# Ten of the eighteen projections of the dilated attention as five units of seven half-size products

## The chip, the cores and the metric

The kernel runs on one core of a Trainium2 chip. The metric is device time in microseconds (us) from the first to the last instruction, with what lies around them. Five engines work side by side, each through its own list of instructions in a fixed order: TensorE (PE in the profile, with its weight loads as PEld), VectorE (DVE), ScalarE (ACT), GpSimd (POOL) and SyncE (SP), which here only issues transfers.

## The reference

A two-layer encoder over 512 tokens of width 1024. The first layer feeds two head groups from one projection; the change concerns group B:

```
z = rmsnorm(x, mix_norm_ab[i]) @ w_in_ab[i]
o_a = mla_mixer(z[..., :IN_A], mla_q_norm[i], mla_kv_norm[i], w_uq, w_ukv, cos_t, sin_t)
o_b = dilated_mixer(z[..., IN_A:], slopes)
x = x + jnp.concatenate([o_a, o_b], axis=-1) @ w_out_ab[i]
...
# dilated_mixer: h_b columns are [q | k | v], each ordered (group, slot, dim): 3 groups, 4 slots, 64 dims
outs.append(o); lses.append(lse)          # one banded attention for each of the 3 groups
comb = sum(softmax(lses)[..., None] * outs)
```

Everything is in float32. The second layer has grouped-query attention, and each layer ends in a SwiGLU FFN.

## The kernel before, in words

Activations lie transposed: a tile holds 128 of the 1024 features in its partitions and the 512 tokens in its columns; eight such tiles make the input of a projection. Each float32 operand is split into a high part (rounded, by ACT) and a low part (the rest, a subtraction on DVE or POOL), and a product is three matmuls, high by high, high by low and low by high (`mm3`, L166 to L168). A projection of 128 output columns (`proj`) is thus 8 x 3 = 24 matmuls with 512 columns each. Its weights come by `load`: one transfer into one of two `wraw` tiles, a cast on ACT (`whi`, L155), a subtraction on POOL (`wlo`, L156).

At the start the input is turned on PE, scaled and split into `x0` to `x15` (`Norm.feed`, L208 and L209). Each tile is also squared on ACT (L199), and POOL adds the squares up into `nacc` (L203). From that sum comes the norm's row factor: four short matmuls sum over the partitions (`rsqrt`, L221), DVE adds the epsilon (L224), POOL raises to the power -0.5 (`rcol`, L226), PE spreads the factor over all partitions (`spread`, L233), and ACT copies it to `rbc` (L237). Only then can a projection's result leave PSUM, since the instruction that takes it out multiplies it by `rbc` (L408, L415, L458, L463, L470, L473, L477). While `rbc` is missing, the banks of PSUM fill up: `BANKS` gives two banks to "acc", two to "s", three to "pt" and one to "o".

The order of the work: the latent projections of head group A (two in the first phase, three by `wblock`); then for each of two values of `sp` the nine projections of the dilated attention (q, k, v for three groups; 128 columns are two slots), then the eight score tiles of these two slots (`steps.tile`, which has a higher priority). After that come group A's heads, the output projection and the FFN. The program is written in this order, but the framework then orders each engine's instructions by a timeline of its own, so that later projections stand between earlier score tiles.

The FFN already works by units of seven (class `Seven`): two projections over 1024 features are a 2 x 2 block product and are formed from seven products of half the depth (4 tiles) and half the columns (256), 7 x 4 x 3 = 84 matmuls with 256 columns, out of sums of the weights (`sab`, `sdc`, split on ACT and DVE) and sums of the activations (`sums`, made once for a set of units).

Of the kernel before, what the change touches and what calls it, by code (L numbers as in the profile page):

```python
# [94 lines left out]
def encoder_kernel(ctx: ExitStack, tc: tile.TileContext, a, out):  # L95
# [349 lines left out]

    for sp in range(2):
        def block(which, g):
            col = IN_A + 768 * which + g * 256 + sp * P
            return proj(wblock(col), xs)

        q1 = [U(f"d{j}", F32R) for j in range(2)]
        k1 = [U(f"d{2 + j}", F32R) for j in range(2)]
        k2 = [U(f"d{4 + j}", F32R) for j in range(2)]
        v0 = [U(f"d{10 + b}", F32R).rearrange("p (c j d) -> p c j d", c=2, j=2) for b in range(2)]
        qf, kf, vf = {}, {}, {}
        o = block(0, 0)
        e = E()
        nc.vector.scalar_tensor_tensor(e, o, 0.125, rbc, op0=ALU.mult, op1=ALU.mult)  # L458
        for j in range(2):
            stack(q1[j], e, j)  # L460
        o = block(1, 0)
        e = E()
        nc.vector.tensor_mul(e, o, rbc)  # L463
        for j in range(2):
            stack(k1[j], e, j)
            swap(k2[j], k1[j])
        for g in (1, 2):
            o = block(0, g)
            qf[g] = U(f"d{5 + g}")
            nc.vector.scalar_tensor_tensor(qf[g], o, 0.125, rbc, op0=ALU.mult, op1=ALU.mult)  # L470
            o = block(1, g)
            kf[g] = U(f"d{7 + g}")
            nc.vector.tensor_mul(kf[g], o, rbc)  # L473
        for g in range(3):
            o = block(2, g)
            e = E()
            nc.vector.tensor_mul(e, o, rbc)  # L477
            pt = psum("pt")
            for c in range(NT):
                nc.tensor.transpose(pt[:, c * P:(c + 1) * P], e[:, c * P:(c + 1) * P], ident)  # L480
            if g == 0:
                pw = pt.rearrange("p (c j d) -> p c j d", c=NT, j=2)
                for b in range(2):
                    split(v0[b][:, :, :, 0:64], v0[b][:, :, :, 64:128], pw[:, 2 * b:2 * b + 2])
            else:
                vf[g] = U(f"d{11 + g}")
                nc.scalar.copy(vf[g], pt)
        if sp == 0:
            finish_latents()
# [177 lines left out]

    H = T // 2  # L670
    NAMES = ("b11", "b21", "b22", "t1", "t2", "t3", "t4")

    def sums(cb, ya, yb, temps, b11, b2, t12_to, t34_to):

        t12, t34 = temps
        nc.vector.tensor_sub(t12[:, 0:H], ya[:, H:T], ya[:, 0:H])
        nc.vector.tensor_sub(t12[:, H:T], yb[:, H:T], t12[:, 0:H])
        nc.vector.tensor_sub(t34[:, 0:H], ya[:, 0:H], t12[:, H:T])
        nc.vector.tensor_sub(t34[:, H:T], yb[:, 0:H], t12[:, H:T])
# [6 lines left out]
        for j, (src, (h, l)) in enumerate(((t12, t12_to), (t34, t34_to))):  # L686
            nc.scalar.activation(h, src, AF.Copy, scale=-1.0)
            nc.vector.scalar_tensor_tensor(l, src, -1.0, h.bitcast(F32), op0=ALU.mult, op1=ALU.subtract)  # L688
            for q in range(2):
                cb[f"t{2 * j + q + 1}"].append((h[:, q * H:q * H + H], l[:, q * H:q * H + H]))  # L690
# [15 lines left out]

    class Seven:

        count = 0

        def __init__(self, loads, cb):
            self.cb = cb
            par = Seven.count % 2
            Seven.count += 1
            self.w = w = len(cb["b11"]) * P
            rg = U("wraw", bufs=2, shape=(P, WCOLS))[:, 0:2 * w]
# [1 line left out]
            at = {"g": rg, "g1": rg[:, 0:w], "g2": rg[:, w:], "u1": u1, "u2": u2}
            for name, v in loads:
                nc.sync.dma_start(at[name].rearrange("p (k n) -> p k n", n=P), v)  # L720
            g1, g2 = at["g1"], at["g2"]
            sab = U("tab", shape=(P, 2, T)).rearrange("p a b -> p (a b)")[:, 0:2 * w]
            sdc = U("bias", shape=(P, 9 * P))[:, 0:2 * w]
# [1 line left out]
            nc.vector.tensor_add(sab[:, 0:w], u1, u2)
            nc.vector.tensor_add(sab[:, w:], sab[:, 0:w], g1)
            self.a = self.parts(sab)
            nc.vector.tensor_add(sdc[:, 0:w], sab[:, w:], g2)
            nc.vector.tensor_add(sdc[:, w:], u1, g1)
            self.d = self.parts(sdc)  # L730
            uh, ul = U("oT", F32R, bufs=2)[:, 0:w], U(("m12", "otmp")[par], F32R)[:, 0:w]
            nc.scalar.copy(uh, u2)  # L732
            nc.gpsimd.tensor_sub(ul, u2, uh.bitcast(F32))  # L733
            self.u = uh, ul

        def parts(self, src):
            hi, lo = (U(t, F32R, bufs=3, shape=(P, WCOLS))[:, 0:2 * self.w] for t in ("whi", "wlo"))
            split(hi, lo, src)
            return hi, lo

        def product(self, o, w, half, name, first):
            n = len(self.cb[name])
            for i in range(n):
                c = slice(half * self.w + i * P, half * self.w + (i + 1) * P)
                x = self.cb[name][i]
                for j, (wt, xp) in enumerate(((w[0], x[0]), (w[0], x[1]), (w[1], x[0]))):
                    nc.tensor.matmul(o[:, 0:H], lhsT=wt[:, c], rhs=xp, start=first and i == 0 and j == 0,  # L747
                                     stop=i == n - 1 and j == 2, skip_group_check=True)

        def run(self, second, third, seventh, fourth):  # L750


            r1, e = psum("s"), U("p", bufs=3, shape=(P, 6 * P))
            self.product(r1, self.g, 0, "b11", True)
            nc.scalar.copy(e[:, 0:H], r1[:, 0:H])
            yield
            r2 = psum("acc")
            self.product(r2, self.g, 1, "b21", True)
            second(r2[:, 0:H], e)
            r3 = psum("pt")  # L760
            self.product(r3, self.a, 0, "t1", True)
            nc.scalar.copy(e[:, T:T + H], r3[:, 0:H])
            self.product(r1, self.a, 1, "t2", False)
            nc.scalar.copy(e[:, H:T], r1[:, 0:H])
            self.product(r3, self.d, 0, "b22", False)
# [404 lines left out]
```

## Time and profile before

| | before |
|---|---|
| median of 3 runs | 1237.79 us (1237.49 to 1238.12) |
| the profiled execution | 1237.33 us, span 1235.4 us |
| PE busy | 1215.1 us, 98% of the span |
| DVE, ACT, POOL busy | 952.4, 682.3, 464.2 us (77%, 55%, 38%) |
| granted clock of TensorE, mean | 0.997 of full speed |

The profile is one execution, recorded by the hardware. Matmuls are pipelined, so that the busy time of PE overlaps itself; what one matmul costs in a stream is read from the starts of its neighbours. A row of a timeline gives start, duration, engine, line, operation and tiles, and in brackets how long the engine sat idle before it and what it waited for.

### The profile page before, as it was taken

What the parts mean: (1) busy time and instruction counts of PE and PEld (TensorE: products, weight loads), DVE (VectorE), ACT (ScalarE), POOL (GpSimd) and SP (SyncE); (2) the same over time, 40 slices, a digit from 0 to 9 for tenths busy, and PEclk for the clock granted to TensorE, in tenths of its full rate; (3) what the DMA queues carried; (4) which work ended last, traced back from release to release, by engine and by line L of the source; (5) the groups of instructions that cost most, each with busy time, mean ns of one, the idle gap of its engine ahead of it and who ended that gap; (6) DMA issues with size and microseconds to landing.
All of it is one profiled execution on the core that took longest, in us unless ns stands there. A gap on an engine that the chain in (4) does not pass through costs nothing.

```text
span 1235.4 us, 20931 instructions
## 1 busy us (share of the span) xinstructions
PE 1215.1 (98%) x7787; PEld 1078.4 (87%) x7787; DVE 952.4 (77%) x1727; ACT 682.3 (55%) x1223; POOL 464.2 (38%) x347
## 2 busy tenths in 40 slices
PE   9999999999999999999999999999999999999997
PEld 7887788777778999999998877787788999999996
DVE  4633437983894999999965768988596799999984
ACT  5424437783653565455545467777454556456554
POOL 4544334444624022111124587756734122111210
PEclk9999999999999999999999999999999999999999
DMA  9343323223213433333424332113232333343331
GB/s 285 95 102 88 92 59 88 79 57 96 85 54 113 118 103 103 103 103 89 118 71 141 99 94 48 44 34 92 73 94 86 111 103 103 104 117 98 103 111 69
DMA packets 204725, 118.20 MB, mean 96 GB/s; under 512 B 17186, under 2 KB 196432, under 8 KB 204624
## 3 DMA queue, kind: packets, MB, share of 16 engines
q1 hardware_dynamic: 202848, 113.70, 32.6%
q10 hardware_dynamic: 1776, 3.17, 0.7%
q8 instruction: 61, 1.00, 0.3%
q14 instruction: 40, 0.33, 0.1%
HBM read 106.09 MB, written 4.19 MB: 89 GB/s over the span
## 4 chain that ended last, share of the span: by engine, by line
PE 84%; DVE 9%; DMA 2%; POOL 2%; issue 1%; ACT 1%; SPq 0%; POOLq 0%; DVEq 0%; ACTq 0%
PE ps_s L747 22%; PE ps_pt L747 11%; PE ps_acc L166 9%; PE ps_acc L167 8%; PE ps_acc L168 8%; PE ps_acc L747 6%; PE ps_pt L352 3%; PE ps_s L168 1%; PE ps_s L166 1%; PE ps_s L167 1%; PE ps_o L380 1%; PE ps_o L379 1%; PE ps_pt L168 1%; DVE b L182 1%; PE ps_pt L166 1%
## 5 line engine op out<-in xcount | busy, mean ns | idle before, releaser
L156 POOL TENSOR_TENSOR wlo<-wraw,whi 128x1024 fp32r<-128x1024 f32 (+3 forms) x99 | 184.9, 1871 | 174.6 <-ACT whi L155 163.2
L155 ACT CAST whi<-wraw 128x1024 fp32r<-128x1024 f32 (+3 forms) x106 | 87.9, 832 | 131.1 <-PE ps_acc L167 69.6
L733 POOL TENSOR_TENSOR m<-m,oT 128x512 fp32r<-128x512 f32 (+1 forms) x26 | 49.0, 1883 | 245.4 <-ACT oT L732 245.4
L166 PE MATMUL ps_acc<-x,whi 128*128 128x512 f32 x280 | 111.6, 401 | 1.9 <-DVE x L371 0.8
L168 PE MATMUL ps_acc<-x,wlo 128*128 128x512 f32 x280 | 112.0, 400 | 0.0
L167 PE MATMUL ps_acc<-x,whi 128*128 128x512 f32 x280 | 111.9, 400 | 0.0
L747 PE MATMUL ps_s<-x,whi 128*128 128x256 f32 x576 | 106.4, 282 | 0.0
L733 POOL TENSOR_TENSOR otmp<-m,oT 128x512 fp32r<-128x512 f32 (+1 forms) x26 | 42.3, 1626 | 153.0 <-ACT oT L732 149.1
L182 DVE TENSOR_TENSOR b<-ps_pt,b 128x512 fp32r<-128x512 f32 x112 | 75.0, 682 | 18.7 <-ACT b L181 18.4
L747 PEld LDWEIGHTS ps_s<-x,whi 128*128 128x128 f32 x576 | 88.8, 188 | 0.4
L181 ACT CAST whi<-bias 128x1024 fp32r<-128x1024 f32 (+1 forms) x52 | 52.8, 1016 | 58.5 <-PE ps_s L747 31.4
L747 PE MATMUL ps_s<-x,wlo 128*128 128x256 f32 x288 | 81.0, 281 | 0.0
L181 ACT CAST b<-ps_pt 128x512 fp32r<-128x512 f32 x112 | 63.7, 585 | 28.1 <-PE ps_pt L352 27.4
L181 ACT CAST whi<-tab 128x1024 fp32r<-128x1024 f32 (+1 forms) x52 | 53.0, 1019 | 46.5 <-PE ps_s L747 36.0
L166 PEld LDWEIGHTS ps_acc<-x,whi 128*128 128x128 f32 x280 | 52.5, 188 | 14.0 <-ACT e L1035 1.2
L182 DVE TENSOR_TENSOR wlo<-bias,whi 128x1024 fp32r<-128x1024 f32 (+1 forms) x52 | 61.1, 1176 | 4.1 <-ACT whi L181 3.4
L182 DVE TENSOR_TENSOR wlo<-tab,whi 128x1024 fp32r<-128x1024 f32 (+1 forms) x52 | 62.5, 1202 | 2.2 <-ACT whi L181 2.2
L182 DVE TENSOR_TENSOR wlo<-wraw,whi 128x1024 fp32r<-128x1024 f32 (+1 forms) x52 | 63.0, 1211 | 0.7 <-ACT whi L181 0.7
L167 PEld LDWEIGHTS ps_acc<-x,whi 128*128 128x128 f32 x280 | 52.7, 188 | 12.3 <-POOL x L373 0.5
L181 ACT CAST whi<-wraw 128x1024 fp32r<-128x1024 f32 (+1 forms) x52 | 52.8, 1015 | 18.2 <-PE ps_acc L167 8.6
L168 PEld LDWEIGHTS ps_acc<-x,wlo 128*128 128x128 f32 x280 | 52.8, 188 | 11.4
L747 PE MATMUL ps_pt<-x,whi 128*128 128x256 f32 x288 | 54.3, 282 | 1.8 <-DVE x L688 1.8
(497 smaller groups left out, 4015.5 us busy)
## 6 DMA issues: line engine op xcount, KB each, us to landing
wraw<-in_ffn_w_in_dram SPq DMA_DIRECT2D x52, 512.0 KB, 3.8
m<-in_ffn_w_in_dram SPq DMA_DIRECT2D x72, 256.0 KB, 3.3
wraw<-in_w_in_ab_dram SPq DMA_DIRECT2D x21, 512.0 KB, 3.9
wraw<-in_ffn_w_out_dram SPq DMA_DIRECT2D x40, 256.0 KB, 2.8
m<-in_ffn_w_out_dram SPq DMA_DIRECT2D x16, 256.0 KB, 3.5
wraw<-in_gqa_w_q_dram SPq DMA_DIRECT2D x8, 512.0 KB, 4.0
m<-in_ffn_w_out_dram SPq DMA_DIRECT2D x16, 192.0 KB, 3.4
wraw<-in_ffn_w_out_dram SPq DMA_DIRECT2D x16, 192.0 KB, 2.9
```

The source lines that it names most:

```text
L155: nc.scalar.copy(h, r)
L156: (low or nc.gpsimd).tensor_sub(l, r, h.bitcast(F32))
L166: nc.tensor.matmul(dst, lhsT=lhs[0], rhs=rhs[0], start=first, stop=False)
L167: nc.tensor.matmul(dst, lhsT=lhs[0], rhs=rhs[1], start=False, stop=False)
L168: nc.tensor.matmul(dst, lhsT=lhs[1], rhs=rhs[0], start=False, stop=last)
L181: nc.scalar.copy(hi, src)
L182: nc.vector.tensor_sub(lo, src, hi.bitcast(F32))
L352: nc.tensor.transpose(pt[:, k * P:(k + 1) * P], p[:, k * P:(k + 1) * P], ident)
L379: nc.tensor.matmul(o, lhsT=vs[k][:, h, :], rhs=pth[:, k, :], start=k == 0, stop=False)
L380: nc.tensor.matmul(o, lhsT=vs[k][:, h, :], rhs=ptl[:, k, :], start=False, stop=k == NT - 1)
L733: nc.gpsimd.tensor_sub(ul, u2, uh.bitcast(F32))
L747: nc.tensor.matmul(o[:, 0:H], lhsT=wt[:, c], rhs=xp, start=first and i == 0 and j == 0, stop=i == n - 1 and j == 2, skip_group_check=True)
```

## The change

The eighteen projections of the dilated attention were nine for `sp` 0, then nine for `sp` 1. Now the first two (q and k of group 0 for `sp` 0) stay as they are, ten others become five units of `Seven`, all written ahead of the first score tile (`PAIRS`), and six of `sp` 1 stay where they were. Three of the ten belong to `sp` 1 (`EARLY_W`); their results wait in `first` and `nacc`. The sums of the activations that the units need are made by the new `window_inputs`, which adds high and low part of `x` again on POOL (`ya`, `yb`), forms four differences of 128 x 256 on DVE for each of four pairs of tiles, and splits them into the `B` tiles. The tables `tab` and `bias` lend their place to the sums of the weights; `tab` is loaded a second time later. In these units POOL, not DVE, makes the low part of the raw weights (`away`).

```diff
     class Seven:
...
-        def __init__(self, loads, cb):
+        def __init__(self, loads, cb, us=None, ut=None):
...
-            u1, u2 = (U(f"m{4 + 2 * par + j}")[:, 0:w] for j in range(2))
+            us = us or [[f"m{4 + 2 * p + j}" for j in range(2)] for p in range(2)]
+            u1, u2 = (U(t)[:, 0:w] for t in us[par])
...
-            self.g = self.parts(rg)
+            self.g = self.parts(rg, ut is not None)
...
+    def window_inputs():
+        cb = {n: [] for n in NAMES}
+        for i in range(4):
+            (ah, al), (bh, bl) = xs[i], xs[i + 4]
+            ya, yb = (U("p", bufs=3, shape=(P, 6 * P))[:, 0:T] for _ in range(2))
+            nc.gpsimd.tensor_add(ya, ah.bitcast(F32), al.bitcast(F32))
+            nc.gpsimd.tensor_add(yb, bh.bitcast(F32), bl.bitcast(F32))
...
+            mixed(ya, yb, temps)
+            mixed_parts(cb, temps, (b[:, 0], b[:, 1]), (b[:, 2], b[:, 3]))
+        return cb
...
+    EARLY_W = ((0, 1), (1, 1), (0, 2))
+    PAIRS = (((0, 0, 1), (0, 1, 1)), ((0, 0, 2), (0, 1, 2)),
+             ((0, 2, 0), (0, 2, 1)), ((0, 2, 2), (1, 0, 1)), ((1, 1, 1), (1, 0, 2)))
...
+        def second(o, e):
+            nc.vector.tensor_add(ra[:, 0:H], o, e[:, 0:H])
+
+        def third(o, e):
+            nc.vector.tensor_add(ra[:, H:T], o, e[:, H:T])
+            nc.vector.scalar_tensor_tensor(ra, ra, sa, rbc, op0=ALU.mult, op1=ALU.mult)
+            wa.take(which_a, ga, ra)
+
+        def seventh(o, e):
+            nc.vector.tensor_add(rb[:, H:T], o, e[:, T:T + H])
+            nc.vector.scalar_tensor_tensor(rb[:, H:T], rb[:, H:T], -sb_, rbc[:, H:T], op0=ALU.mult, op1=ALU.mult)
+
+        def fourth(o, e):
+            nc.vector.scalar_tensor_tensor(rb[:, 0:H], o, -sb_, rbc[:, 0:H], op0=ALU.mult, op1=ALU.mult)
+            wb.take(which_b, gb, rb)
...
+    wcb = window_inputs()
+    open_ = None
+    windows[0].block(0, 0)
+    windows[0].block(1, 0)
+    for one, other in PAIRS:
+        unit = window_unit(one, other, wcb)
+        next(unit)
+        if open_ is not None:
+            for _ in open_:
+                pass
+        else:
+            finish_latents()
+        next(unit)
+        open_ = unit
```

The order in which the engines work changes at three places of the first 65 us. On POOL, between the first sums of squares and the factor: here the order of before, from the second sum to the power (`nacc_152` is the sum of squares of the input's norm, `rcol_354` its factor, `wlo` low parts of weights).

```order
L203 TENSOR_TENSOR nacc_152<-nacc_152,e_206 128x512
L203 TENSOR_TENSOR nacc_152<-nacc_152,e_219 128x512
L156 TENSOR_TENSOR wlo_381<-wraw_379,whi_380 128x1024
L156 TENSOR_TENSOR wlo_417<-wraw_415,whi_416 128x1024
L203 TENSOR_TENSOR nacc_152<-nacc_152,e_232 128x512
L203 TENSOR_TENSOR nacc_152<-nacc_152,e_245 128x512
L203 TENSOR_TENSOR nacc_152<-nacc_152,e_258 128x512
L156 TENSOR_TENSOR wlo_455<-wraw_453,whi_454 128x1024
L226 TENSOR_TENSOR rcol_354<-tiny_352,mhalf_79 128x4
```

In the changed kernel the last twelve rows ahead of the same power are these (L547 and L548 are the additions of `window_inputs`, L482 the low part of a unit's last weights).

```order
L482 TENSOR_TENSOR d19_827<-d15_804,d18_826 128x512
L203 TENSOR_TENSOR nacc_152<-nacc_152,e_232 128x512
L548 TENSOR_TENSOR p_548<-x6_148,x14_149 128x512
L156 TENSOR_TENSOR wlo_455<-wraw_453,whi_454 128x1024
L547 TENSOR_TENSOR p_561<-x3_142,x11_143 128x512
L203 TENSOR_TENSOR nacc_152<-nacc_152,e_245 128x512
L548 TENSOR_TENSOR p_562<-x7_150,x15_151 128x512
L482 TENSOR_TENSOR d17_681<-m12_658,d16_680 128x512
L156 TENSOR_TENSOR wlo_578<-wraw_576,whi_577 128x1024
L203 TENSOR_TENSOR nacc_152<-nacc_152,e_258 128x512
L156 TENSOR_TENSOR wlo_615<-wraw_613,whi_614 128x1024
L226 TENSOR_TENSOR rcol_354<-tiny_352,mhalf_79 128x4
```

From the sum with `e_206` to the last one, with `e_258`, two rows stood between the sums. Now there are thirteen: seven of the eight additions, both L482 and four low parts. One low part stands between the last sum and the power, as before.

On PE, where the sum is taken over the partitions: before, a projection's matmuls stand behind it (`ps_pt_385` and `ps_pt_421` are latent projections).

```order
L221 MATMUL ps_o_343<-ones_77,e_271 128x1
L166 MATMUL ps_pt_385<-x7_150,whi_380 128x512
L167 MATMUL ps_pt_385<-x15_151,whi_380 128x512
L168 MATMUL ps_pt_385<-x7_150,wlo_381 128x512
L166 MATMUL ps_pt_421<-x0_136,whi_416 128x512
L167 MATMUL ps_pt_421<-x8_137,whi_416 128x512
```

In the changed kernel the same sum stands behind all of `ps_pt_385`, `ps_pt_421` and the third latent projection, `ps_acc_459`, and the spreading directly behind it, with the first projection of the dilated attention (`ps_acc_582`) next.

```order
L168 MATMUL ps_acc_459<-x7_150,wlo_455 128x512
L221 MATMUL ps_o_343<-ones_77,nacc_152 128x1
L221 MATMUL ps_o_343<-ones_77,e_271 128x1
L221 MATMUL ps_o_343<-ones_77,nacc_152 128x1
L221 MATMUL ps_o_343<-ones_77,e_271 128x1
L221 MATMUL ps_o_343<-ones_77,nacc_152 128x1
L221 MATMUL ps_o_343<-ones_77,e_271 128x1
L221 MATMUL ps_o_343<-ones_77,nacc_152 128x1
L221 MATMUL ps_o_343<-ones_77,e_271 128x1
L233 MATMUL ps_o_356<-ident_72,rcol_354 128x128 x4
L166 MATMUL ps_acc_582<-x0_136,whi_577 128x512
```

On DVE, ahead of the same place (L224, `tiny_352`, adds the epsilon; `first_566` and `b3_567` are the last differences of `window_inputs`, `bias_663` is a sum of the first unit's weights, of which one part comes by the transfer into `wraw_656`):

```order
L527 TENSOR_TENSOR otmp_565<-p_562,otmp_565 128x256
L528 TENSOR_TENSOR first_566<-p_561,otmp_565 128x256
L529 TENSOR_TENSOR first_566<-p_562,otmp_565 128x256
L535 SCALAR_TENSOR_TENSOR b3_567<-otmp_565,b3_567 128x512
L535 SCALAR_TENSOR_TENSOR b3_567<-first_566,b3_567 128x512
L475 TENSOR_TENSOR bias_663<-m5_657,wraw_656 128x512
L224 TENSOR_SCALAR tiny_352<-ps_o_343 128x4
L408 TENSOR_TENSOR oT_364<-ps_acc_276,rbc_361 128x512
```

Before, L224 followed on the last copy of the input (L286 `e_273`). Now all 24 instructions of `window_inputs` and one weight sum stand ahead of it.

## Rows read from the trace of the kernel before

**Rows 1.** The page: busy time of each engine, share of the span, instructions.

```profile
PE 1215.1 (98%) x7787; PEld 1078.4 (87%) x7787; DVE 952.4 (77%) x1727; ACT 682.3 (55%) x1223; POOL 464.2 (38%) x347
```

**Rows 2.** Timeline of PE, 31 to 47 us: start, duration, what.

```profile
31.80 0.28 PE L221 MATMUL ps_o<-ones,nacc 128*128 128x1 f32 x2
...
33.73 0.48 PE L166 MATMUL ps_pt<-x,whi 128*128 128x512 f32 x1
...
39.62 1.05 PE L233 MATMUL ps_o<-ident,rcol 128*128 128x128 f32 x8
40.43 0.48 PE L167 MATMUL ps_pt<-x,whi 128*128 128x512 f32 x1
...
40.98 0.40 PE L166 MATMUL ps_acc<-x,whi 128*128 128x512 f32 x1
...
46.58 0.40 PE L166 MATMUL ps_acc<-x,whi 128*128 128x512 f32 x1
```

**Rows 3.** Chain that ended last, in the FFN: start, duration, what.

```profile
516.68 2.82 PE ps_s L747 x24
519.50 1.42 PE ps_pt L747 x12
...
526.60 2.82 PE ps_s L747 x24
```

**Rows 4.** The page's groups: the weight loads of these matmuls.

```profile
L747 PEld LDWEIGHTS ps_s<-x,whi 128*128 128x128 f32 x576 | 88.8, 188 | 0.4
```

**Rows 5.** Timeline of POOL, 13 to 54 us.

```profile
18.79 1.31 POOL L203 TENSOR_TENSOR nacc<-nacc,e 128x512 f32<-128x512 f32 x1 [1.31 <-ACT e L199]
...
24.76 4.05 POOL L203 TENSOR_TENSOR nacc<-nacc,e 128x512 f32<-128x512 f32 x3
...
34.14 1.04 POOL L226 TENSOR_TENSOR rcol<-tiny,mhalf 128x4 f32<-128x4 f32 x1 [2.97 <-DVE tiny L224]
...
48.12 2.40 POOL L156 TENSOR_TENSOR wlo<-wraw,whi 128x1024 fp32r<-128x1024 f32 x1
50.48 1.74 POOL L203 TENSOR_TENSOR nacc<-nacc,e 128x512 f32<-128x512 f32 x1
```

**Rows 6.** Timeline of DVE, 17 to 61 us.

```profile
17.55 0.74 DVE L209 SCALAR_TENSOR_TENSOR x<-ps_pt,gcol,x 128x512 fp32r<-128x512 f32 x1
...
33.90 0.16 DVE L224 TENSOR_SCALAR tiny<-ps_o 128x4 f32<-128x4 f32 x1 [3.73 <-PE ps_o L221]
41.34 0.69 DVE L408 TENSOR_TENSOR oT<-ps_acc,rbc 128x512 f32<-128x512 f32 x1 [7.27 <-ACT rbc L237]
...
48.39 2.68 DVE L209 SCALAR_TENSOR_TENSOR m<-e,gcol,m 128x512 fp32r<-128x512 f32 x1 [0.80 <-ACT m L208]
...
60.26 0.69 DVE L463 TENSOR_TENSOR e<-ps_acc,rbc 128x512 f32<-128x512 f32 x1
```

**Rows 7.** One DVE line of the FFN, 340 to 660 us: duration ns min/median/max.

```profile
L833 DVE TENSOR_TENSOR m<-m,m x18: 404/416/1181, 389.9 to 637.5; 128x256 f32<-128x256 f32 x18
```

**Rows 8.** The page's issues of transfers: KB each, us from issue to landing.

```profile
wraw<-in_w_in_ab_dram SPq DMA_DIRECT2D x21, 512.0 KB, 3.9
```

**Rows 9.** Timeline, chain and stretch (clock third from the right) near 367 us.

```profile
367.45 0.39 PE L747 MATMUL ps_pt<-x,whi 128*128 128x256 f32 x1 [1.83 <-DVE x L688]
...
368.42 2.93 PE ps_pt L747 x12
...
368.00:370.00 2.00, 1.80 (x9) 1.58 (x8) 1.16 (x3) 2.00 (x6) 1.87 (x2) 0.51 0.00 0
```

**Rows 10.** The FFN, 460 to 580 us: DVE and POOL groups (busy us, mean ns), and the stretch.

```profile
L182 DVE TENSOR_TENSOR wlo<-tab,whi 128x1024 fp32r<-128x1024 f32 x12 | 14.6, 1213 | 0.8 <-ACT whi L181 0.8
L726 DVE TENSOR_TENSOR tab<-tab,wraw 128x512 f32<-128x512 f32 x12 | 8.2, 681 | 0.1
...
460.00:580.00 120.00, 119.60 (x1007) 119.19 (x1006) 117.33 (x180) 66.39 (x109) 21.53 (x12) 1.00 0.36 102
```

**Rows 11.** The score tiles of both `sp`, 83 to 218 us: PE, PEld, DVE, ACT, POOL busy.

```profile
83.00:218.00 135.00, 134.93 (x694) 106.98 (x693) 62.25 (x168) 62.00 (x133) 55.25 (x38) 1.00 0.32 83
```

More of the change, by code (lines that the diff above doesn't have):

```diff
@@ L443, in encoder_kernel @@
     hd0 = Heads([(f"d{b}", f"d{4 + b}") for b in range(4)] + [("d16", "d17"), ("d18", "d19")])
-    for sp in range(2):
[L447 to L489, printed above, removed]
@@ new lines, in window_inputs @@
+    def window_inputs():
[5 more added lines that the diff above has]
+            nc.gpsimd.tensor_add(yb, bh.bitcast(F32), bl.bitcast(F32))
+            if i % 2:
+                temps = U("otmp"), U("first")
+            else:
+                t = U("bias", shape=(P, 9 * P))
+                temps = t[:, 0:T], t[:, T:2 * T]
+            b = B(i)
+            cb["b11"].append((ah[:, 0:H], al[:, 0:H]))
+            cb["b21"].append((bh[:, 0:H], bl[:, 0:H]))
+            cb["b22"].append((bh[:, H:T], bl[:, H:T]))
+            mixed(ya, yb, temps)
+            mixed_parts(cb, temps, (b[:, 0], b[:, 1]), (b[:, 2], b[:, 3]))
+        return cb
@@ new lines, in encoder_kernel, with window_unit @@
+    EARLY_W = ((0, 1), (1, 1), (0, 2))
+    PAIRS = (((0, 0, 1), (0, 1, 1)), ((0, 0, 2), (0, 1, 2)),
+             ((0, 2, 0), (0, 2, 1)), ((0, 2, 2), (1, 0, 1)), ((1, 1, 1), (1, 0, 2)))
+    windows = [Window(0), Window(1)]
+    windows[0].lay()
+    def window_unit(one, other, cb):
+        (wa, which_a, ga), (wb, which_b, gb) = one, other
+        wa, wb = windows[wa], windows[wb]
+        ca, cc = wa.column(which_a, ga), wb.column(which_b, gb)
+        v = [("g", wview(wab, 0, KB, ca, ca + P))]
+        v += [(f"u{h + 1}", wview(wab, 4 * h, 4 * h + 4, cc, cc + P)) for h in range(2)]
+        ra, rb = wa.place(which_a, ga), wb.place(which_b, gb)
+        sa, sb_ = (0.125 if which == 0 else 1.0 for which in (which_a, which_b))
+        def second(o, e):
[10 more added lines that the diff above has]
+            wb.take(which_b, gb, rb)
+        unit = Seven(v, cb, (("m5", "m12"), ("d14", "d15")), (("d16", "d17"), ("d18", "d19")))
+        return unit.run(second, third, seventh, fourth)
@@ new lines, in encoder_kernel @@
+    wcb = window_inputs()
[8 more added lines that the diff above has]
+                pass
+        else:
+            finish_latents()
+        next(unit)
+        open_ = unit
+    for _ in open_:
+        pass
+    for sp in range(2):
+        win = windows[sp]
+        if sp == 1:
+            win.lay()
+            for g in range(3):
+                for which in range(2):
+                    if (which, g) not in EARLY_W:
+                        win.block(which, g)
+            for g in range(3):
+                if (2, g) not in EARLY_W:
+                    win.block(2, g)
+        q1, k1, k2, v0, qf, kf, vf = win.q1, win.k1, win.k2, win.v0, win.qf, win.kf, win.vf
@@ L617, in mla_head @@
             steps.tile(lambda: first(c), lambda p, c=c: turn(p, pth, ptl, c), end if c == NT - 1 else None)
+    tab = U("tab", shape=(P, 2, T))
+    nc.sync.dma_start(tab, a["c_mla"])
     ptiles = rotate(PM)
@@ L664, in mix_last @@
         nr.feed(xt[KB - 1], gain(g, KB - 1))
-    H = T // 2
-    NAMES = ("b11", "b21", "b22", "t1", "t2", "t3", "t4")
     def sums(cb, ya, yb, temps, b11, b2, t12_to, t34_to):
[L675 to L679, printed above, removed]
+        mixed(ya, yb, temps)
         split(*b11, ya[:, 0:H])
@@ L685, in sums @@
         cb["b22"].append((h[:, H:T], l[:, H:T]))
[L686 to L690, printed above, removed]
+        mixed_parts(cb, temps, t12_to, t34_to)
     def combine(xt, rb, gk):
@@ L705, in combine @@
         return cb
-    class Seven:
-        count = 0
-        def __init__(self, loads, cb):
[L712 to L716, printed above, removed]
-            u1, u2 = (U(f"m{4 + 2 * par + j}")[:, 0:w] for j in range(2))
[L718 to L723, printed above, removed]
-            self.g = self.parts(rg)
[L725 to L765, printed above, removed]
-            third(r3[:, 0:H], e)
-            self.product(r1, self.d, 1, "t3", False)
-            seventh(r1[:, 0:H], e)
-            yield
-            self.product(r1, self.u, 0, "t4", False)
-            fourth(r1[:, 0:H], e)
```

116 lines of the change are left out of this document (added).

## The prediction

> **What bounds the kernel now.** I read the page first: PE is busy for 98% of the span [rows 1]. That alone says little, since matmuls overlap in these rows, so the next view is the timeline of PE in the stretch that the change touches, and there the starts. From 40.98 to 46.58 us lies one projection, 24 matmuls of 512 columns: 5.60 us, 0.233 each [rows 2]. In the FFN's stretch of the chain the same instruction of successive units starts at 516.68 and 526.60 us: 9.92 us for a unit of 84 half-size matmuls, 0.118 each, and a product of twelve takes 1.42 [rows 3]. In both stretches starts follow one another at one pace: PE is fed, and what it need not do is time won, up to the point where something else is late. The list of waits (which engine waited for whom) names none of PE between 10 and 110 us. The third view is then what must be ready for PE at given moments. For the start that is the norm's row factor, and the timelines of POOL and DVE show its way: the last sum of squares ends at 28.8 us (24.76 + 4.05), the epsilon is added at 33.90, the power ends at 35.18 [rows 5, 6], the spreading starts at 39.62 and PE has projections in between [rows 2]. The factor is early and covered.
>
> **The matmuls.** Ten projections go, 10 x 5.60 = 56.0 us; five units come, 5 x 9.92 = 49.6. That is 6.4 us off PE. The price of the units is that of rows 3, where weights are loaded as often as here. The Trainium skill (TensorE: Matmul & The Clock Gate, section Back-to-back issue gap) speaks against such a change: it says that weight loads set the spacing as well, with 81 ns for 128 columns and 131 ns for 512, so that half the columns would not be half the time. By those figures the removed 240 matmuls would be 31.4 us and the new 420 at least 34.0, an estimate of 2.6 us lost on PE. The rows here have 118 and 233 ns, and I take them.
>
> **The factor comes late.** POOL's new order puts thirteen other instructions between the sums of squares, and everything in its queue waits its turn. I follow it from 18.3 us, where the fifth tile's low part is there (17.55 + 0.74 [rows 6]), which the first of these additions needs. From that addition to the last sum there are 13 instructions of 128 x 512 at 1.31 us and four low parts at 2.40 [rows 5]: 17.0 + 9.6 = 26.6 us, so 44.9 at the earliest.
>
> They will not run so, since DVE and POOL stand in each other's way. DVE's L209 at 48.39 takes 2.68 us where one with a source in PSUM takes 0.74; it ends at 51.07, which is 0.55 behind the end of POOL's low part (48.12 + 2.40); and POOL's next sum, issued at 50.48, takes 1.74 in place of 1.31 [rows 5, 6]. Both are instructions with two sources in SBUF: such a DVE instruction lets a running POOL instruction finish, then goes ahead of the next one, which pays 0.43. Half-size ones do the same: L833 has a median of 416 ns and a longest of 1181 [rows 7]. The new differences and splits on DVE are all of this kind. Seventeen of them fall between these POOL instructions, 6 of full and 11 of half size. At 0.43 for a full one and 0.43 x 416 / 681 = 0.26 for a half one (0.681 is L726 [rows 10]) they add 5.5 us: the last sum ends near 50.4.
>
> Then DVE must clear its queue ahead of the epsilon. While POOL makes one more low part (2.40 + 0.26, to 53.1), DVE waits or gets one half-size instruction in; after it come three half-size (1.2) and two full splits and the weight sum L475 (2.0), so near 56.4 with 0.1 between them. L475 also needs a transfer that can start only when POOL has done with the low part ahead of the last sum, near 48.9, and lands 3.9 us after its issue [rows 8]: it is there. Epsilon 0.16, power 1.04, and 0.3 between them as before: 57.9. From the start of the spreading to the end of L408, which frees the first bank, 41.34 + 0.69 - 39.62 = 2.4 us [rows 2, 6]. The first projection of the dilated attention then starts at **60.3 us**; without a stall it starts at 46.58. PE can do nothing in between: it has done all three latent projections, and the two "acc" banks, both "s" and two "pt" hold results that wait for the factor. So 13.7 us are lost, and the cover (projections behind the sum) is gone.
>
> The bounds: with no blocking at all the low part ahead of the last sum ends at 43.6, the transfer lands at 47.5, L475 (0.7) and epsilon end at 48.4, the power at 49.5, L408 at 51.9: 5.3 us lost. If each DVE instruction cost POOL its whole length (0.68 or 0.42), it is 3.1 us more than I take: 16.8.
>
> **The clock.** After PE idled 1.83 us at 365.6 us its granted clock was 0.51 in the following stretch, the lower of the two levels (1.2 GHz), and twelve half-size matmuls took 2.93 us instead of 1.42 [rows 9]. Up to there it had been busy, at the full level (2.4 GHz). A stall of several us should bring the same: 1.5 us, with 0 and 3.0 (two stalls) as the bounds.
>
> **The units' supply.** After L408 DVE has a long list ahead of the first unit's third product. The list up to the last L429 took from 41.34 to 60.26 before, 18.9 us [rows 6], with POOL in its way more often than now; two weight sums (0.68 each), L474 (0.68) and the split (1.21 [rows 10]) come to it. PE has two projections, two products and small sums to do, 2 x 5.6 + 2 x 1.42 + 0.8 = 14.8, and 1.5 for the clock. Between no wait, if blocking nearly ends, and 18.9 + 3.3 - 16.3 = 5.9. Thereafter a unit costs DVE four sums (2.7), two splits (2.4), five half-size operations (2.1) and one full one (0.7), 7.9 us against PE's 9.92. In the FFN DVE carries more (117.33 of 120 us busy) and PE keeps its pace [rows 10]. I take 1 us in all.
>
> **The score tiles.** Three projections, 16.8 us, leave the stretch in which they filled PE between score tiles. DVE is busy there for 62.3 of 135 us, ACT for 62.0 and POOL for 55.3 [rows 11]; over the 118 us that are left that is 53%, 53% and 47%, so what covers the tiles' waits is still there. Nothing, bound 3 us.
>
> **The sum.** The profiled execution took 1237.33 us (span 1235.4 and 1.9 around it), 0.46 under the median. 1237.33 - 6.4 + 13.7 + 1.5 + 1.0 + 0 = **1247.1 us**.
>
> **The rivals.** (1) The other side: the factor isn't delayed by POOL, because the additions fall into POOL's waits for ACT, and the sum is ready when PE comes to it. Then only the lost cover costs: the third latent projection ends at 46.58 less the sums (33.73 - 31.80) and the spreading (40.43 - 39.62), 43.8; sums to 45.7, factor 1.45 after them as before, and 2.4 to L408 make 49.6, a stall of 3.0 and 1237.33 - 6.4 + 3.0 = 1233.9. It decides where the last sum ends: at 43.8 us or earlier. Against it: POOL's instructions alone, unblocked, reach 44.9. (2) Blocking is small: 5.3 instead of 13.7, 1238.7. For it speaks only that POOL may be waiting anyway; against it the rows at 48 us. (3) DVE sets the units' pace: each POOL instruction of a unit (2.40 + 1.31) holds DVE up in full, 7.9 + 3.7 = 11.6 per unit, and the start of the list is 5 us late; 1.7 x 4 + 5.0 in place of 1.0 gives 1257.9, half of it 1252.5. (4) The score tiles run short of cover: 1250.1. (5) The spacing is bound by weight loads, of 188 ns each [rows 4]: 84 x 0.188 = 15.8 per unit, 79 us in place of 49.6, 1276.5. Rows 3 exclude it for units of the same shape, where loads overlap.
>
> **How the numbers follow.** The forecast with its own range (1243 to 1251, from one clock loss more or less and 3 us at the factor) has 0.55, rival 1 has 0.09, rival 2 0.15, rival 3 0.15, rival 4 0.05, rival 5 0.01. The range for eight in ten reaches down to rival 2 and up to rival 3: 1238 to 1258. A change of 0.2% (2.5 us) is about what a measurement of this kernel can tell. Faster is rival 1, 0.09. Within it lies most of rival 2, 0.11. Slower is the rest, 0.80.
>
> **What the profile after would show.** PE with an idle stretch ending near 60 us, its releaser DVE L408's counterpart; the power on POOL ending near 58 and the last sum of squares near 50; DVE's new differences at 1 us and more where POOL is busy; a stretch of PEclk near 0.5 behind the idle one; units of 9.9 to 10 us without waits; score tiles with PE at one pace. The prediction is wrong if the power ends by 50 us, or if PE waits again by several us inside the units or between the score tiles.

## The result, and the profile after

The changed kernel takes 1253.67 us (median of 4 runs, 1252.93 to 1254.75) against 1237.93 us beside it: a ratio of 1.0131 (95% interval 1.0119 to 1.0143), 15.7 us slower. The forecast was 1247.1, in a range of 1238 to 1258. Of the forecast's terms two came out near what was worked out (one of them in part by luck), the other three were too small, the units' supply most of all.

The page shows 180 more instructions on PE, 1.4 us more busy time, and a span that is 17.6 us longer [rows 1] (the profiled execution is the longest of the four):

```profile
PE 1216.5 (97%) x7967; PEld 1087.6 (87%) x7967; DVE 1021.8 (82%) x1801; ACT 699.2 (56%) x1256; POOL 476.1 (38%) x355
```

POOL's timeline around the factor, which answers to [rows 5] (start, duration, what, idle time before and its releaser):

```profile
17.69 1.30 POOL L548 TENSOR_TENSOR p<-x,x 128x512 f32<-128x512 f32 x1 [0.89 <-DVE x L209]
...
21.73 1.27 POOL L203 TENSOR_TENSOR nacc<-nacc,e 128x512 f32<-128x512 f32 x1 [1.49 <-ACT e L199]
...
35.43 1.41 POOL L548 TENSOR_TENSOR p<-x,x 128x512 f32<-128x512 f32 x1 [1.55 <-DVE first L528]
...
46.22 2.85 POOL L156 TENSOR_TENSOR wlo<-wraw,whi 128x1024 fp32r<-128x1024 f32 x1
49.03 1.47 POOL L203 TENSOR_TENSOR nacc<-nacc,e 128x512 f32<-128x512 f32 x1
50.46 2.56 POOL L156 TENSOR_TENSOR wlo<-wraw,whi 128x1024 fp32r<-128x1024 f32 x1
55.78 1.04 POOL L226 TENSOR_TENSOR rcol<-tiny,mhalf 128x4 f32<-128x4 f32 x1 [2.76 <-DVE tiny L224]
```

The last sum of squares ends at 50.5 us (forecast 50.4), the power at 56.8 (forecast 57.9; before, 35.2). DVE at the same place, against [rows 6]:

```profile
46.73 2.62 DVE L526 TENSOR_TENSOR otmp<-p 128x256 f32<-128x256 f32 x1
...
50.82 2.49 DVE L528 TENSOR_TENSOR first<-p,otmp 128x256 f32<-128x256 f32 x1
...
55.55 0.15 DVE L224 TENSOR_SCALAR tiny<-ps_o 128x4 f32<-128x4 f32 x1
59.60 0.69 DVE L408 TENSOR_TENSOR oT<-ps_acc,rbc 128x512 f32<-128x512 f32 x1 [3.90 <-ACT rbc L237]
```

L526 (2.62 us where 0.41 is its length alone) ends at 49.35, which is 0.28 us behind the end of POOL's low part (46.22 + 2.85), and L528 ends 0.29 us behind the next one: two-source instructions of DVE that stand still while POOL runs, and the epsilon L224 is queued behind them. On PE [rows 2]:

```profile
53.18 0.36 PE L221 MATMUL ps_o<-ones,e 128*128 128x1 f32 x2
56.87 2.08 PE L233 MATMUL ps_o<-ident,rcol 128*128 128x128 f32 x8 [3.33 <-POOL rcol L226]
60.35 0.79 PE L166 MATMUL ps_acc<-x,whi 128*128 128x512 f32 x1 [1.40 <-DVE oT L408]
...
66.49 0.43 PE L168 MATMUL ps_acc<-x,wlo 128*128 128x512 f32 x1
66.76 0.39 PE L166 MATMUL ps_acc<-x,whi 128*128 128x512 f32 x1
```

The first dilated projection starts at 60.35 us instead of 46.58, 13.8 us late. Behind it the clock is at the lower level (0.50 in the first row below, third number from the right): from 60.35 to 66.76 us lie fifteen matmuls, 6.41 us, where fifteen at 0.233 take 3.50. That is 2.9 us.

Stretches of the trace: length, then busy time of PE, PEld, DVE, ACT, POOL (instructions), granted clock, share of transfers:

```profile
60.00:62.00 2.00, 1.65 (x4) 1.36 (x5) 2.00 (x4) 1.65 (x3) 0.31 (x1) 0.50 0.00 0
90.00:120.00 30.00, 25.53 (x208) 24.71 (x208) 29.10 (x37) 11.95 (x21) 14.86 (x6) 1.00 0.20 54
```

The second row lies in the middle of the five units: PE is fed for 25.5 of 30 us, DVE is busy for 29.1. The list of waits, 60 to 215 us (total, times, longest):

```profile
PE ps_s L497 <- DVE d L642: 2.2, 2, 1.1
PE ps_acc L166 <- DVE x L182: 1.9, 1, 1.9
...
PE ps_pt L595 <- DVE e L642: 1.2, 1, 1.2
PE ps_s L497 <- DVE d L638: 1.1, 1, 1.1
```

The waits for L642 and L638 (4.5 us, between 91 and 121 us) stand inside the units: PE waits for a bank of PSUM that DVE has not emptied. The one for L182 stands between the last score tiles, at 213.65 us. Why DVE is late in the units, POOL (first two rows) and DVE show:

```profile
91.42 4.53 POOL L488 TENSOR_TENSOR wlo<-wraw,whi 128x1024 fp32r<-128x1024 f32 x1 [6.02 <-ACT whi L487]
95.92 1.73 POOL L482 TENSOR_TENSOR d<-m,d 128x512 fp32r<-128x512 f32 x1
...
93.60 0.42 DVE L630 TENSOR_TENSOR d<-ps_acc,p 128x256 f32<-128x256 f32 x1
93.94 2.56 DVE L474 TENSOR_TENSOR bias<-tab,wraw 128x512 f32<-128x512 f32 x1
96.42 1.77 DVE L475 TENSOR_TENSOR bias<-m,wraw 128x512 f32<-128x512 f32 x1
98.12 0.41 DVE L642 SCALAR_TENSOR_TENSOR d<-ps_s,rbc 128x256 f32<-128x256 f32 x1
```

The weight sums L474 and L475 take 2.56 and 1.77 us where 0.68 is their length, the first beside POOL's L488, the second beside its L482; L642, for which PE waits, is queued behind both.

### The profile page after: what moved, and what is told of

The parts are those of the page before. It is cut to its first block, busy times and chain, and to the rows that moved or that the text cites. A ratio compares the mean times of both kernels' runs of the same rounds, so it can differ in the third digit from the quotient of the medians.

```text
span 1253.0 us, 21439 instructions
## 1 busy us (share of the span) xinstructions
PE 1216.5 (97%) x7967; PEld 1087.6 (87%) x7967; DVE 1021.8 (82%) x1801; ACT 699.2 (56%) x1256; POOL 476.1 (38%) x355
## 4 chain that ended last, share of the span: by engine, by line
PE 75%; DVE 16%; issue 3%; ACT 3%; POOL 2%; DMA 1%; SPq 1%; POOLq 0%; ACTq 0%; DVEq 0%
PE ps_s L497 21%; PE ps_pt L497 11%; PE ps_acc L166 7%; PE ps_acc L167 7%; PE ps_acc L168 6%; PE ps_acc L497 5%; PE ps_pt L352 3%; DVE wlo L488 2%; PE ps_o L380 1%; PE ps_s L168 1%; PE ps_s L166 1%; PE ps_s L167 1%; PE ps_o L379 1%; DVE b L182 1%; DVE bias L474 1%
## 5 line engine op out<-in xcount | busy, mean ns | idle before, releaser
L156 POOL TENSOR_TENSOR wlo<-wraw,whi 128x1024 fp32r<-128x1024 f32 (+3 forms) x89 | 162.4, 1827 | 132.3 <-ACT whi L155 116.1
L482 POOL TENSOR_TENSOR otmp<-m,oT 128x512 fp32r<-128x512 f32 (+1 forms) x26 | 48.5, 1866 | 245.5 <-ACT oT L481 245.5
L155 ACT CAST whi<-wraw 128x1024 fp32r<-128x1024 f32 (+3 forms) x96 | 77.4, 810 | 97.2 <-PE ps_acc L167 45.0
L497 PE MATMUL ps_s<-x,whi 128*128 128x256 f32 x616 | 114.8, 284 | 2.2 <-DVE d L642 2.2
L482 POOL TENSOR_TENSOR m<-m,oT 128x512 fp32r<-128x512 f32 (+1 forms) x26 | 42.4, 1630 | 153.6 <-ACT oT L481 149.7
L497 PEld LDWEIGHTS ps_s<-x,whi 128*128 128x128 f32 x616 | 95.7, 190 | 3.3 <-DVE d L642 2.6
L182 DVE TENSOR_TENSOR b<-ps_pt,b 128x512 fp32r<-128x512 f32 x112 | 75.0, 683 | 13.1 <-ACT b L181 12.8
L166 PE MATMUL ps_acc<-x,whi 128*128 128x512 f32 x200 | 81.4, 410 | 3.7 <-DVE oT L408 1.4
L167 PE MATMUL ps_acc<-x,whi 128*128 128x512 f32 x200 | 81.0, 405 | 0.0
L168 PE MATMUL ps_acc<-x,wlo 128*128 128x512 f32 x200 | 80.7, 404 | 0.0
L488 DVE TENSOR_TENSOR wlo<-tab,whi 128x1024 fp32r<-128x1024 f32 (+1 forms) x57 | 68.7, 1205 | 5.5 <-ACT whi L487 5.5
L488 DVE TENSOR_TENSOR wlo<-bias,whi 128x1024 fp32r<-128x1024 f32 (+1 forms) x57 | 67.3, 1181 | 4.0 <-ACT whi L487 3.1
L487 ACT CAST whi<-wraw 128x1024 fp32r<-128x1024 f32 (+1 forms) x57 | 58.0, 1017 | 18.3 <-PE ps_acc L167 8.6
L488 DVE TENSOR_TENSOR wlo<-wraw,whi 128x1024 fp32r<-128x1024 f32 (+1 forms) x52 | 63.1, 1213 | 0.8 <-ACT whi L487 0.8
L497 PE MATMUL ps_pt<-x,whi 128*128 128x256 f32 x328 | 61.8, 282 | 1.8 <-DVE x L535 1.8
L497 PEld LDWEIGHTS ps_s<-x,wlo 128*128 128x128 f32 x308 | 58.3, 189 | 0.0
L497 PE MATMUL ps_s<-b,whi 128*128 128x256 f32 x304 | 56.7, 280 | 0.0
L497 PE MATMUL ps_s<-d,whi 128*128 128x256 f32 x288 | 55.1, 281 | 0.0
```

The source lines that it names most:

```text
L155: nc.scalar.copy(h, r)
L156: (low or nc.gpsimd).tensor_sub(l, r, h.bitcast(F32))
L166: nc.tensor.matmul(dst, lhsT=lhs[0], rhs=rhs[0], start=first, stop=False)
L167: nc.tensor.matmul(dst, lhsT=lhs[0], rhs=rhs[1], start=False, stop=False)
L168: nc.tensor.matmul(dst, lhsT=lhs[1], rhs=rhs[0], start=False, stop=last)
L182: nc.vector.tensor_sub(lo, src, hi.bitcast(F32))
```

## The experiments

**Undoing POOL's part at the start.** In the first run the additions come behind the power, in the second DVE makes them.

```diff
+            with tc.issue_after(norm.power):
                 nc.gpsimd.tensor_add(ya, ah.bitcast(F32), al.bitcast(F32))
                 nc.gpsimd.tensor_add(yb, bh.bitcast(F32), bl.bitcast(F32))
```

> The changed kernel, with the eight additions of window_inputs put behind the power of the input's norm on POOL (nothing is left out). Theory (POOL's order makes the factor late): the last sum of squares ends by 38 us instead of 50.5, the power by 44 instead of 56.8, the first dilated projection starts between 46.6 and 50 instead of 60.35, and the early wait of TensorE near 20 to 26 us goes. The differences then come behind the factor, so that a wait of 0 to 8 us opens ahead of the first unit's third product. Time 1237 to 1246, most likely 1240. Rival A (what is late is DVE's and POOL's work for the units as a whole, and it is only moved): the wait comes back in full ahead of the first unit's third product, 1250 to 1254. Rival B (the factor is held by the units' other low parts): the power stays at 50 us or later, 1250 to 1254.

Measured: 1259.02 us, ratio 1.0171 (1.0153 to 1.019), slower than the change. The power ends at 40.9 us and the first dilated projection starts at 52.77 instead of 60.35, so the additions, and the differences that follow from them, did make the factor late. But the same work now meets the list of DVE behind the factor. From 50 to 100 us:

```profile
50.00:100.00 50.00, 37.24 (x208) 33.25 (x206) 49.75 (x67) 24.53 (x38) 21.91 (x13) 0.83 0.24 64
```

DVE is full, PE is fed for 37 of 50 us, at a clock of 0.83. Rival A held by its mechanism; the time lies 5 us above its range, and the early wait, which the theory saw gone, is there (3.25 us).

```diff
-            nc.gpsimd.tensor_add(ya, ah.bitcast(F32), al.bitcast(F32))
-            nc.gpsimd.tensor_add(yb, bh.bitcast(F32), bl.bitcast(F32))
+            nc.vector.tensor_add(ya, ah.bitcast(F32), al.bitcast(F32))
+            nc.vector.tensor_add(yb, bh.bitcast(F32), bl.bitcast(F32))
```

> The changed kernel, with the eight additions of window_inputs on DVE instead of POOL (nothing is left out). Theory (POOL's queue is the chain that ends last): seven instructions of 1.31 to 1.74 us leave it, 9 to 12 us, and DVE gets eight of 0.7 to 1.2 us, 6 to 9 us, ahead of the epsilon; the last sum of squares ends near 41 us and DVE decides; the first dilated projection starts at 53 to 57 us, the time is 1246 to 1251. Rival (DVE's list ahead of the epsilon is the chain): the factor is later than in the changed kernel, start at 62 to 68 us, 1255 to 1262.

Measured: 1247.21 us, 1.0076 (1.0054 to 1.0097), 6.5 us less than the change: as the theory had it, with the power at 51.3 us. PE waits for the factor for only 0.95 us, and the time is still 9.5 us above the kernel before: an early wait (3.66 us, see below) and waits in the units are left. Eight instructions of 1.31 us and more on POOL cost more than eight on DVE, although DVE is the busier engine.

**Parts alone, in the kernel before.** The additions alone, then all of `window_inputs`; their results are used by nothing.

```diff
+    for i in range(4):
+        (ah, al), (bh, bl) = xs[i], xs[i + 4]
+        ya, yb = (U("p", bufs=3, shape=(P, 6 * P))[:, 0:T] for _ in range(2))
+        nc.gpsimd.tensor_add(ya, ah.bitcast(F32), al.bitcast(F32))
+        nc.gpsimd.tensor_add(yb, bh.bitcast(F32), bl.bitcast(F32))
```

> The kernel before, with only the eight additions of window_inputs added on POOL; their results are used by nothing. Theory (each instruction in POOL's queue ahead of the factor counts): POOL needs 8 times 1.31 to 1.74 us more, the power ends at 45 to 48 us instead of 35.2, the cover of projections takes up most of it, TensorE waits 2 to 6 us behind the latent projections: 1240 to 1245. Rival (the additions fall into POOL's waits for ACT): the power ends by 40 us, 1238 as before.

Measured: 1244.62 us, 1.0051 (1.0036 to 1.0066), 6.9 us more than before, just at the theory's upper end. Its start on PE:

```profile
47.91 2.08 PE L233 MATMUL ps_o<-ident,rcol 128*128 128x128 f32 x8 [3.00 <-POOL rcol L226]
51.38 0.79 PE L166 MATMUL ps_acc<-x,whi 128*128 128x512 f32 x1 [1.40 <-DVE oT L408]
```

It is 4.8 us late (46.58 before); of the other 2 us, 1.5 are the lower clock behind the stall (seven matmuls take 3.13 us, 51.38 to 54.51, where seven at 0.233 take 1.63).

```diff
+    window_inputs()
```

> The kernel before, with all of window_inputs added (additions on POOL, differences and splits on DVE and ACT); its results are used by nothing, and all eighteen projections stay plain. Theory (the inputs alone make the factor late): the first dilated projection starts near 58 to 60 us, and nothing is won by units, so 1238 + 13.7 + 1.5 to 2.5 for the clock = 1252 to 1255, which makes the units themselves worth about nothing (the 6.4 us off TensorE go to waits inside them). Rival (a large part of the lateness comes from the units' own weights, L475, L482 and L488): the projection starts near 50 to 54 us, 1243 to 1248.

Measured: 1254.8 us, 1.0135 (1.0118 to 1.0152). So the inputs alone cost 17.1 us, as much as the whole change:

```profile
24.50 0.50 PE L167 MATMUL ps_acc<-x,d 128*128 128x512 f32 x1 [3.25 <-DVE x L209]
...
58.34 2.07 PE L233 MATMUL ps_o<-ident,rcol 128*128 128x128 f32 x8 [7.06 <-POOL rcol L226]
61.81 0.79 PE L166 MATMUL ps_acc<-x,whi 128*128 128x512 f32 x1 [1.40 <-DVE oT L408]
```

The theory held, though the start lies 2 us behind its range, and the rival (the units' own weights make the factor late) fell. The first row is an early wait, here without any transfer of the units' weights.

**Inside the units.** Low parts of the units' weights, all on POOL, or none of the large ones on POOL (in the change one of three).

```diff
-            self.a = self.parts(sab)
+            self.a = self.parts(sab, ut is not None)
...
-            self.d = self.parts(sdc)
+            self.d = self.parts(sdc, ut is not None)
```

> The changed kernel, with all low parts of the units' weights on POOL (before, two of the three were on DVE). Nothing is left out. Theory A (DVE's own busy time bounds units two to four): DVE loses 2 x 1.2 us per unit, the waits of 5 us inside the units go, 1247 to 1250. Theory B (it is POOL's instructions with two sources in SBUF that hold DVE up, 2.4 us each): two more of them per unit, waits stay or grow, 1253 to 1262.

Measured: 1261.79 us, 1.0192 (1.0175 to 1.0209), 8.1 us more than the change.

```diff
-            self.g = self.parts(rg, ut is not None)
+            self.g = self.parts(rg)
```

> The changed kernel, with no low part of the units' weights of 1024 columns on POOL: the one of the raw weights goes to DVE too. Nothing is left out. Theory A (DVE's own busy time bounds the units): 1.2 us more on DVE per unit, units two to five each lose about that, 1256 to 1259. Theory B (POOL holds DVE up): one POOL instruction of 2.4 us less per unit, waits shrink, 1248 to 1252.

Measured: 1248.28 us, 1.0083 (1.0068 to 1.0098), 5.4 us less than the change, though DVE has 1.2 us more to do in each unit. Theory B, in both. The group of L474 from 70 to 120 us (count, busy time, mean ns) in the changed kernel:

```profile
L474 DVE TENSOR_TENSOR bias<-tab,wraw 128x512 f32<-128x512 f32 x5 | 11.1, 2219 | 0.0
```

With the low part on DVE:

```profile
L474 DVE TENSOR_TENSOR bias<-tab,wraw 128x512 f32<-128x512 f32 x5 | 3.4, 682 | 0.0
```

The first dilated projection starts no earlier here (61.05 us), so the gain lies behind the factor. The stretch 90 to 120 us of that run:

```profile
90.00:120.00 30.00, 30.00 (x254) 29.79 (x253) 25.65 (x42) 15.19 (x25) 8.46 (x3) 1.00 0.27 71
```

PE is fed for all of the 30 us and starts 254 matmuls in place of 208. The Trainium skill (SBUF — State Buffer, section SBUF: two separate sides) says that DVE, with two sources in SBUF, and GpSimd share one pair of ports by an exclusive lock, held for a whole instruction. The rows agree: 2219 ns with POOL's 2.4 us instruction beside it, 682 without.

**Units without inputs.** Both runs leave out the sums of the activations.

```diff
-            nc.gpsimd.tensor_add(ya, ah.bitcast(F32), al.bitcast(F32))
...
-            mixed_parts(cb, temps, (b[:, 0], b[:, 1]), (b[:, 2], b[:, 3]))
+            for n, (h, l) in zip(NAMES[3:], ((ah, al), (bh, bl), (ah, al), (bh, bl))):
+                cb[n].append((h[:, H:T], l[:, H:T]))
```

> The changed kernel without the sums of the activations: the additions, differences and splits of window_inputs are left out, and the units take halves of x itself in their place, so that the matmuls are as many and as large. Theory (the inputs cost 17 us and the units about nothing, and the two add up): 1253.7 - 17.1 = 1236.6, range 1234 to 1239, with the first dilated projection at 47 to 49 us. Rival (the units' own weights make the factor late too, or the units stall without the inputs' delay ahead of them): 1241 to 1247.

Measured: 1240.4 us, 1.0024 (1.0014 to 1.0034): between the theory and the rival. No wait for the factor is left, but an early one of 3.2 us (below) with the lower clock behind it, and 1.9 us of waits for L488 inside the units. The same with the low parts on DVE and the weights' transfers later:

> The units alone: the changed kernel with the sums of the activations left out (additions, differences and splits; the units take halves of x in their place), all low parts of the units' weights on DVE, and the transfers of their weights behind that of the third latent projection. As many and as large matmuls as in the changed kernel. Theory (the five units are worth 6.4 us less on TensorE and run without waits once POOL leaves DVE alone): 1237.8 - 6.4 = 1231.4, with up to 2 us of small waits, 1230.5 to 1234. Rival A (a unit costs more than 9.92 us here, or the score tiles behind lack the cover of the projections that left them): 1235 to 1238. Rival B (DVE holds the first unit up even without the inputs): a wait of 3 us and more before 80 us, with a clock loss, 1236 to 1240.

Measured: 1230.71 us, 0.9945 (0.993 to 0.9959), 6.6 us less than before (5.1 to 8.7 by the interval). The theory's 6.4 us are there once nothing holds the units up:

```profile
60.00:90.00 30.00, 30.00 (x254) 30.00 (x254) 29.87 (x50) 15.68 (x26) 1.51 (x1) 1.00 0.47 123
90.00:120.00 30.00, 30.00 (x216) 27.88 (x215) 20.94 (x33) 12.83 (x21) 8.12 (x4) 1.00 0.32 92
```

DVE is as full as in the change (29.87 of 30), POOL is nearly idle up to 90 us, and PE does not wait.

**Towards a version that wins.** All new work on DVE, the additions behind the last copy of the input:

```diff
-            nc.gpsimd.tensor_add(ya, ah.bitcast(F32), al.bitcast(F32))
+            with tc.issue_after(fed):
+                nc.vector.tensor_add(ya, ah.bitcast(F32), al.bitcast(F32))
...
-            self.g = self.parts(rg, ut is not None)
+            self.g = self.parts(rg)
...
-            nc.gpsimd.tensor_sub(ul, u2, uh.bitcast(F32))
+            (nc.gpsimd if ut is None else nc.vector).tensor_sub(ul, u2, uh.bitcast(F32))
```

> The changed kernel with none of the new work on POOL: the additions go to DVE, behind the last copy of the turned input (L286), and all low parts of the units' weights go to DVE too. Nothing is left out. Theory (POOL's new instructions do the harm, through its own queue ahead of the factor and by holding DVE up in the units): the power ends by 42 us instead of 56.8, DVE uses its idle stretch of 30 to 40 us, no wait of 1 us and more inside the units; the gains of the two single moves add up, 1253.7 - 6.5 - 5.4 = 1241.8, range 1237 to 1246. Rival (DVE, with all of it, becomes the bound): 1247 to 1254.

Measured: 1247.03 us, 1.0072 (1.0059 to 1.0085), the rival's side: the two gains do not add up. From 80 us on the units run with one wait of 0.4 us, but the power ends at 53.4 us:

```profile
45.01 8.39 POOL L226 TENSOR_TENSOR rcol<-tiny,mhalf 128x4 f32<-128x4 f32 x1 [3.51 <-DVE tiny L224]
```

It takes 8.39 us instead of 1.04, and it ends 0.9 us behind the end of a row of DVE instructions that stand back to back and all have two sources in SBUF:

```profile
44.78 0.14 DVE L224 TENSOR_SCALAR tiny<-ps_o 128x4 f32<-128x4 f32 x1
44.85 0.40 DVE L528 TENSOR_TENSOR first<-p,otmp 128x256 f32<-128x256 f32 x1
...
52.08 0.41 DVE L529 TENSOR_TENSOR first<-p,otmp 128x256 f32<-128x256 f32 x1
```

This run also has an early wait on PE, as the change and the other runs up to here with units or with all inputs have (2.6 to 3.7 us for the longest one):

```profile
23.71 1.09 PE L283 MATMUL ps_pt<-ident,b 128*128 128x128 f32 x4 [3.26 <-DVE e L286]
```

Next, the transfers of the units' weights come behind that of the third latent projection's:

```diff
+                with tc.issue_after(raw_loads[2]):
                     nc.sync.dma_start(at[name].rearrange("p (k n) -> p k n", n=P), v)
```

> The kernel of the run before this one (all new work on DVE), with the transfers of the units' weights put behind the one of the third latent projection's weights in SP's queue. Nothing is left out. Theory (these early transfers, ahead of which ACT waits to issue its stores, make the wait of 3.4 us near 20 us and the half clock behind it): the wait and the half clock go, 2 to 5 us less than without the move, 1234 to 1241. Rival (that wait has another cause): within 1.5 us of the run without the move.

Measured: 1243.86 us (1241.31 to 1247.01), 1.0049 (1.0034 to 1.0064), 3.2 us less, in the median: four of its six runs lie below all five of the run before, two lie among them. The time is above the theory's range of 1234 to 1241, but the early wait is gone, as it had it, and the clock is 1.00 from 20 to 30 us. How the transfers made it (ACT's stores stood still in its queue) was not tried apart. They are not the only thing that can make it: the inputs alone had one, behind DVE. What is left is DVE from 30 to 80 us, full, with PE fed for 43.5 of 50:

```profile
30.00:80.00 50.00, 43.50 (x233) 37.38 (x233) 49.55 (x77) 24.32 (x39) 14.68 (x8) 0.90 0.34 91
```

Three units in place of five, with four more plain projections ahead of them, first with the additions on POOL behind the power, then in the form of the last run:

```diff
-    PAIRS = (((0, 0, 1), (0, 1, 1)), ((0, 0, 2), (0, 1, 2)),
-             ((0, 2, 0), (0, 2, 1)), ((0, 2, 2), (1, 0, 1)), ((1, 1, 1), (1, 0, 2)))
+    PAIRS = (((0, 2, 0), (0, 2, 1)), ((0, 2, 2), (1, 0, 1)), ((1, 1, 1), (1, 0, 2)))
```

> The changed kernel with three units instead of five (the first two pairs are plain projections again, ahead of the units), the additions and the units' weights behind the power of the input's norm, and the differences behind the last instruction that takes a latent projection out of PSUM (L415). Nothing is left out. Theory (what costs is the place of the new work: it stands ahead of the factor on POOL and DVE, and five units in a row leave DVE no slack): the power ends by 38 us, TensorE waits by at most 3 us up to 80 us, DVE has six projections' time, 33 us, for its new 20 us of work, and three units save 3 x 1.28 = 3.8 us: 1234 to 1240. Rival (the new DVE and POOL work costs TensorE its time wherever it stands ahead of the score tiles): waits of 6 us and more between 45 and 110 us, 1243 to 1250.

> The same, with three units instead of five: the first two pairs are plain projections, ahead of the units. Nothing is left out. Theory A (DVE's work ahead of the first unit is the rest of the loss, and four plain projections give it 22 us of time): less than with five units although 2.6 us more matmuls stay, 1233 to 1237. Theory B (DVE keeps up with five units): 1 to 4 us more than with five units.

Measured: 1251.69 us, 1.0109 (1.0094 to 1.0124), and 1245.05 us, 1.0064 (1.0051 to 1.0078). Both have waits of the kind of the first one's rival, and the first run's time lies 2 us above that rival's range. Between 45 and 110 us PE stands idle for 5.9 us in the one and 4.1 in the other, where the rival had 6 and more: 3.6 us behind L534 on ACT, which takes its inputs from DVE, in the one, 4.1 us for DVE to take out a projection (L612) in the other. That the second is 1.2 us above five units fits theory B by the number, but the single runs overlap (1244.14 to 1249.25 against 1241.31 to 1247.01), and its reason does not hold, since DVE does not keep up in either. No version that makes the sums of the activations beat the kernel before.

## Why the prediction was right, and where not

**The matmuls, -6.4 us: right.** The units alone measured -6.6. The other estimate of that paragraph, 2.6 us lost on PE, is out.

**The factor, +13.7 us: right by its way; that the size fits to 0.1 us is in part luck.** The last sum of squares ends at 50.5 and PE starts at 60.35, 13.8 us late. But POOL began its row at 17.69, not 18.3; on the way it waited 3.4 us for ACT and DVE (the two rows above and one of 0.36), for which the prediction had nothing; and what blocking added to the 26.6 us was about 2.8, not 5.5. From the last sum to the end of the power it took 6.3 us where 7.5 were worked out, and from the spreading to the end of L408 3.4 where 2.4 were, since the spreading itself ran at the lower clock (2.08 us; 1.05 before [rows 2]; granted clock 0.50). These errors cancel. The additions are part of the loss (6.9 us with the clock, when alone), the rest comes with the differences and splits (17.1 in all, when alone).

**The clock, +1.5 us: too small here.** Fifteen full-size matmuls ran at the lower level behind the stall, 2.9 us, near the upper bound of 3.0. The length of the stall does not explain it: with all low parts on POOL the same two waits (3.33 and 1.40 us) were followed by only seven such matmuls, 3.01 us in place of 1.63, which is 1.4 lost.

```profile
60.30 0.79 PE L166 MATMUL ps_acc<-x,whi 128*128 128x512 f32 x1 [1.40 <-DVE oT L408]
...
63.31 0.39 PE L167 MATMUL ps_acc<-x,whi 128*128 128x512 f32 x1
```

So this term differs between executions by as much as it was mis-sized, and why is open.

**The units' supply, +1.0 us: mis-sized, the step that failed.** It set 7.9 us of DVE work against 9.92 of PE, and compared with the FFN, where DVE carries more and PE keeps its pace [rows 10]. The wait ahead of the first unit, for which it had 5.9 as the bound, did not come. Inside the units PE waited for 4.7 us, in four pieces of 1.1 to 1.2 and one of 0.2, which the prediction had named as a sign of being wrong. The work was counted without what POOL adds: 2.4 us for the low part of the raw weights in each unit, during which a weight sum of DVE stands still (L474, 2219 ns for 682). Moving that one instruction gave 5.4 us back. That was rival 3, priced at 5.4 (half of it) to 10.8 us above the forecast; it should have been part of the sum, since the blocking had been counted for the factor.

**The score tiles, 0: a little too small.** One wait that the kernel before has not stands between the last of them, 1.87 us at 213.65, within the bound of 3. The units alone have it too (1.85), and 6.6 us arrive at the end all the same; with the raw low part on DVE it is 0.4 us, so the three missing projections alone do not set it.

In the profiled execution -6.4, 13.8, 2.9 and 4.7 add up to 15.0 of the 17.6 us by which the span grew, with that wait to 16.9; the rest was not taken apart. The runs with one part each give -6.6 + 17.1 (inputs alone, clock included) + 5.4 = 15.9 us, where 15.7 were measured, but parts do not simply add up here: the units without inputs and the inputs alone would make 1240.4 + 17.1 = 1257.5, 3.8 more than the change, and the gains of two single moves did not add up either. So the closeness of that sum shows little. What the prediction did not have at all is the early wait between 20 and 26 us (2.70 and 1.55 us on PE). What it costs there was not tried. PE's sums end at 53.54 us, 2 us before DVE comes to the epsilon, so PE's own delay did not make the factor later; with all new work on DVE the move that took the wait away was worth 3.2 us.
